# Order of the bank copies and of the late products in a hand-ordered down projection (gated linear attention layer with MLP, one Trainium2 core)

## The chip, the cores and the metric

The kernel runs on one core of a Trainium2 chip. The metric is the device time of one execution in microseconds (us); the time given for a kernel is the median of its runs. Five engines work side by side, each through its own instructions in the order in which they were queued: PE (TensorE, matrix products), DVE (VectorE) and ACT (ScalarE) for work on elements, POOL (GpSimd), and SP, which here issues the loads. They wait for one another by semaphores. PE reads its operands from SBUF, the on-chip memory of 128 partitions, and accumulates into PSUM, which has 8 banks of 128 x 512 float32.

## The reference

One layer with 256 tokens of width 2048, all in float32: RMS norm, gated linear attention, residual; RMS norm, an MLP with squared ReLU and 8192 hidden columns, residual; a last RMS norm.

```python
def _sq_relu_mlp(h, w_up, w_down):
    a = jax.nn.relu(h @ w_up)
    return (a * a) @ w_down

def reference(x, ...):
    h = x
    h = h + _gla_mixer(_rmsnorm(h, gla_norm[0]), ...)
    h = h + _sq_relu_mlp(_rmsnorm(h, mlp_norm[0]), mlp_w_up[0], mlp_w_down[0])
    return _rmsnorm(h, final_norm)
```

The change touches the product with `w_down` alone, and the final norm that follows it.

## The kernel before

**Precision.** A float32 product is made of three products of a reduced type (float32r): each operand is split into a high part, the value cast by ACT (`copy_hi`, line 110), and a low part, the rest, by DVE (`parts`, line 119): high x high, high x low, low x high. So each weight tile that comes by DMA costs ACT a cast, DVE a subtraction, and PE three times the matmuls. One matmul streams 256 columns; a load of weights goes beside the matmul before it. The split parts stand in five slots of the pool `wpool` (tags `hi` and `lo`), the raw tiles in six.

**The MLP.** The hidden columns go in 8 rounds (`ROUNDS`, m = 0 to 7) of 1024. `up` (line 679) makes the activations of a round in two passes (q = 0, 1) of 8 up steps each, into two banks that it takes from the queue `free`. An up step is one weight tile of 128 x 1024 and 24 matmuls (line 195). When a pass has ended, its `end` runs behind the first split of the next pass: `normalized` (DVE, `su`), then `forms`, which squares on ACT and writes, with DVE and ACT, up to eight stationary forms of each of the round's four pairs kp, each split into high and low part (`act`). Once in a round (`even`, step 3 of the pass q = 0) `weights` lays the two halves of an up step's weights further apart (`gap`).

`down` (line 776) adds a round's part of the second product to `h`. It goes over the output in groups g of 512 columns (`GROUPS` = 4), in an order that turns with each round, so that the last group of a round is the first of the next; consecutive passes over one group share their banks. The last round takes only groups 0 and 1 there. For each group there are four pairs kp, that is four steps, 16 in a round. A step is of one of two kinds:

- plain: one weight tile of 128 x 1024, 24 matmuls into the banks B32 and BX4, which hold the two token tiles of the group;
- by sums (`by_sums`, line 667): a 2 x 2 scheme with seven block products in place of eight, 21 matmuls. The tile's first 256 columns aren't split (so 128 x 768). Three products (9 matmuls) use the tile's own blocks. DVE makes four sums of blocks (line 821: one instruction over 512 columns, two over 256), which are split in turn, and four more products (12 matmuls) use them, into P57, P16 and BX4. P57 and P16 are banks of their own; what they hold is kept in `sums` between a group's passes, and `combine` adds it to `h` in the end.

94 steps go by sums: in the last round those with odd kp; before it all but kp = 0, and kp = 0 too where a round goes on with the group of the last one.

**Order.** The program interleaves the two generators: 18 up steps lead; then `down` yields once in each step, between its first products and those of the sums, and one up step is put in there. With 128 up steps the last ten of the 120 steps of `down` (numbers 110 to 119) have none. Each engine keeps the order that the build's scheduler gave it from the program and from `tc.issue_after`, which holds an instruction behind another: line 741 holds every copy of `copy_end` behind the last cast.

**Banks at a change of group.** Of the eight banks, four hold a group, two an up pass. In the last step of a group (`last`), ahead of its products, ACT copies `h` into two free banks for the next group's B32 and BX4 (`begin`, line 762). The old group's four banks are put into `late`. In the new group's first step by sums (kp = 1), ahead of its products, `settle` copies P16 and B32 out, into `sums` and `h`, and `begin` copies the new P16 in; behind the yield it copies P57 and BX4 out and the new P57 in. So ACT has the three copies of the first lot between the cast of that step's tile and that of the up step, and the three of the second between that and the cast of the sums. All go through line 744.

**The end.** Columns 1024 to 2047 of the last round are done behind `down`, with 8 loads of 128 x 1024 (line 911), whole token tiles as stationary operand, into five accumulators `acc`: four are begun in the last step of `down`, the fifth at kt = 1, where the last group's four banks are settled. The first two loads are used at once, the other six kept and used accumulator by accumulator. `side` and `pump` place small pieces of work (`combine`, `finish`) behind the splits.

Of the kernel before, what the change touches and what calls it, by code (L numbers as in the profile page):

```python
# [33 lines left out]
T = 256  # L34
NT = T // P
D = 2048
# [32 lines left out]
def tile_gla_mlp(ctx, tc, x, xt, cols, w_vg, w_in, w_gate, w_out, w_up, w_down, final_norm, out):  # L69
# [593 lines left out]
    def order_of(m):  # L663

        return range(GROUPS)[:: 1 if m % 2 else -1]

    def by_sums(m, g, kp):

        if m == ROUNDS - 1:
            return g < 2 and kp % 2 == 1  # L670
        return kp > 0 or m > 0 and g == order_of(m)[0]

# [58 lines left out]
    def stationary(m, kp, f):  # L731
        return [acts[m][kp // 2][:, kp % 2, i, f] for i in range(2)]
# [1 line left out]
    left, right = slice(0, T), slice(T, 2 * T)  # L734
    used, begun = set(), set()
    n_sums = [0]
    late = []

    def copy_end(to, src):

# [21 lines left out]
    def begin(k, g):  # L762
        i = free.popleft()
        bank = psum_bank(i)
        if k in (B32, BX4) or g in begun:
            copy_end(two(bank), home(k, g))
            used.add(bank.name)
        return i, bank

    def settle(n=2):  # L770

        for f in late[:n]:
            f()
        del late[:n]

    def down(passes):

        ahead = None
        for n, (m, g) in enumerate(passes):
            fresh = not n or passes[n - 1][1] != g  # L780
            if fresh:
                banks = ahead or {k: begin(k, g) for k in (B32, BX4)}
                if m == ROUNDS - 1:
                    flush()
            ends = n + 1 == len(passes) or passes[n + 1][1] != g
            for kp in range(KP):
                last = ends and kp == KP - 1
                at = lambda f: stationary(m, kp, f)

                def product(k, o, a, w, c):  # L790
# [10 lines left out]
                by_parts = by_sums(m, g, kp)  # L801
                w = parts(raw, 2 * GT, slots(), [(T * by_parts, 2 * GT)])
                if fresh and kp == 1:
                    settle()
                    banks[P16] = begin(P16, g)
                if last:
                    if n + 1 < len(passes):
                        ahead = {k: begin(k, passes[n + 1][1]) for k in (B32, BX4)}
                    else:
                        acc[0][:] = [going_on(psum_bank(free.popleft()), h[:, 0, G + lo : G + hi]) for lo, hi in cuts[0]]  # L810
                        acc[1][:] = [going_on(psum_bank(free.popleft())[:, : hi - lo], h[:, 1, G + lo : G + hi]) for lo, hi in cuts[1][:-1]]
                if by_parts:
                    block = lambda i: slice(i * T, (i + 1) * T)
# [7 lines left out]
                    add = lambda o, x, y: nc.vector.tensor_tensor(o, x, y, op=ALU.add)  # L821

                    with tc.issue_after(last_lo[0].ins):
                        add(u[:, :2], raw[:, :1].to_broadcast([P, 2, T]), raw[:, 1:3])
                        add(u[:, 2], u[:, 0], raw[:, 2])
                        last_sum[0] = add(u[:, 3], u[:, 2], raw[:, 3]).ins
                else:
                    for i in range(2):
                        for k, f in ((B32, (A11, A12)), (BX4, (A21, A22))):
                            product(k, slice(0, GT), at(f[i]), w, slice(i * GT, (i + 1) * GT))  # L830
                yield
                if fresh and kp == 1:
                    settle()
                    banks[P57] = begin(P57, g)
                if by_parts:

                    with tc.issue_after(last_lo[0].ins):
                        wu = parts(wk, G, slots())
                    product(P57, left, at(S1), wu, block(0))
                    product(P57, right, at(S3), wu, block(1))  # L840
                    product(P16, right, at(S2), wu, block(2))
                    product(BX4, right, at(A22), wu, block(3))
            if ends:

                def end(k, i, bank, g=g):
                    copy_end(home(k, g), two(bank))
                    free.append(i)

                late.extend(lambda k=k, end=end, of=banks[k]: end(k, *of) for k in range(4))
                begun.add(g)  # L850
                if m == ROUNDS - 1 or m == ROUNDS - 2 and g > 1:
                    late[-1] = lambda f=late[-1], g=g: (f(), side.extend(combine(g)))

    def combine(g):

# [9 lines left out]
            tt(1, 2, 3, ALU.subtract), tt(0, 0, 3, ALU.add), lambda: put(1),  # L865
        ]


    cuts = [HALF, [(0, 512), (512, 768), (768, 1024)]]
    acc = [[], []]  # L870
    passes = [(m, g) for m in range(ROUNDS) for g in order_of(m) if m < ROUNDS - 1 or g < 2]
    steps = up()
    for _ in range(KT + 2):
        next(steps)
    for _ in down(passes):
        next(steps, None)
# [121 lines left out]
```

## Time and profile before

| | us |
|---|---|
| median of 3 runs | 1080.33 (1080.19 to 1081.63) |
| the profiled execution | 1079.18 |
| its span, first to last instruction | 1077.1 |
| the 120 steps of `down` with the up steps among them | 432.8 to 1045.9 |
| of it the steps without an up step | from 1012.6 |
| last matmul starts | 1068.3 |
| mean granted TensorE clock | 0.998 |

Times within the execution count from the span's start. A row of a timeline gives the start, the duration, the engine, the line, the operation, what it writes and reads, how many equal instructions it stands for, and in brackets the engine's idle time before it with what ended it. Instructions of one engine overlap by their fill and drain, so the distance from start to start, and not the duration, is what one of them takes in a row of others; a matmul shows 0.28 us and the next one starts 0.113 to 0.118 us later. Ends of matmuls are modelled, and a few matmul records are missing.

### The profile page before, as it was taken

To read this page: it belongs to the slowest core of one execution; us is meant where nothing else is said; L and a number is where in the kernel's file an instruction comes from. 1 tells how busy PE (TensorE), PEld (TensorE's weight loads), DVE (VectorE), ACT (ScalarE), POOL (GpSimd) and SP (SyncE) were. 2 spreads that over 40 slices of the span, in tenths; PEclk is the share of its full clock that TensorE was granted. 3 is DMA by queue.
4 is the path that set the end of the run, shared out by engine and by line. 5 is a ranking of instruction groups with operands and counts; after the bars stand their busy time and mean duration, and the time that the engine had idled before them with its cause. 6 is when DMAs were issued, how large, how long until landed. Compare 5 with 4: busy or idle time off the path is not lost.

```text
span 1077.1 us, 22212 instructions
## 1 busy us (share of the span) xinstructions
PE 1061.8 (99%) x9148; PEld 1058.2 (98%) x9148; DVE 834.9 (78%) x1148; ACT 677.0 (63%) x917; POOL 12.8 (1%) x39
## 2 busy tenths in 40 slices
PE   9999999999999999999999999999999999999996
PEld 8999999999999999999999999999999999999986
DVE  5777645646556466898988988988989989889976
ACT  6775444545445455676686676677577667667675
POOL 0000000000000000000000000000000000000000
PEclk9999999999999999999999999999999999999999
DMA  9957765555655556556665565566566566665562
GB/s 338 321 158 214 202 193 157 154 160 176 194 183 189 181 175 193 177 179 208 218 200 196 191 217 180 195 204 209 176 197 222 183 220 195 200 198 194 172 192 107
DMA packets 94788, 210.44 MB, mean 195 GB/s; under 512 B 6704, under 2 KB 7600, under 8 KB 94560
## 3 DMA queue, kind: packets, MB, share of 16 engines
q1 hardware_dynamic: 93728, 206.99, 60.2%
q10 hardware_dynamic: 960, 2.05, 0.5%
q8 instruction: 71, 1.16, 0.4%
q14 instruction: 29, 0.24, 0.1%
HBM read 206.92 MB, written 2.10 MB: 194 GB/s over the span
## 4 chain that ended last, share of the span: by engine, by line
PE 87%; DVE 7%; issue 2%; DMA 2%; ACT 1%; SPq 0%; ACTq 0%; POOLq 0%; POOL 0%; DVEq 0%
PE acc L158 47%; PE up L195 30%; PE acc L195 6%; DVE lo L124 3%; PE aux L195 2%; DVE work L821 2%; ACT hi L114 1%; DVE lo L147 1%; DMA raw<-in_w_vg 1%; PE aux L158 1%; PE aux L564 1%; DMA zz<-in_xt 1%; PE aux L492 1%; DVE act L729 0%; DVE work L721 0%
## 5 line engine op out<-in xcount | busy, mean ns | idle before, releaser
L114 ACT CAST hi<-raw 128x1024 fp32r<-128x1024 f32 (+3 forms) x386 | 373.6, 991 | 173.8 <-PE acc L158 108.5
L158 PE MATMUL acc<-hi,act 128*128 128x256 f32 x1828 | 336.7, 278 | 4.9 <-ACT hi L114 4.8
L124 DVE TENSOR_TENSOR lo<-raw,hi 128x1024 fp32r<-128x1024 f32 (+3 forms) x226 | 246.3, 1092 | 105.7 <-ACT hi L114 105.1
L158 PEld LDWEIGHTS acc<-hi,act 128*128 128x128 f32 x1828 | 279.9, 188 | 7.1 <-ACT hi L114 7.1
L195 PE MATMUL up<-hl,hi 128*128 128x256 f32 x1024 | 280.3, 278 | 0.0
L195 PE MATMUL up<-hh,hi 128*128 128x256 f32 x1024 | 280.3, 278 | 0.0
L195 PE MATMUL up<-hh,lo 128*128 128x256 f32 x1024 | 271.4, 278 | 0.0
L147 DVE TENSOR_TENSOR lo<-raw,hi 128x1024 fp32r<-128x1024 f32 x160 | 195.0, 1220 | 61.9 <-ACT hi L114 61.2
L158 PE MATMUL acc<-lo,act 128*128 128x256 f32 x914 | 225.1, 278 | 0.0
L195 PEld LDWEIGHTS up<-hl,hi 128*128 128x128 f32 x1024 | 192.3, 188 | 0.0
L195 PEld LDWEIGHTS up<-hh,hi 128*128 128x128 f32 x1024 | 192.2, 188 | 0.0
L195 PEld LDWEIGHTS up<-hh,lo 128*128 128x128 f32 x1024 | 186.7, 188 | 0.0
L114 ACT CAST hi<-work 128x1024 fp32r<-128x1024 f32 x94 | 99.5, 1058 | 107.7 <-DVE work L821 95.6
L158 PEld LDWEIGHTS acc<-lo,act 128*128 128x128 f32 x914 | 162.8, 188 | 0.2 <-DVE lo L124 0.2
L124 DVE TENSOR_TENSOR lo<-work,hi 128x1024 fp32r<-128x1024 f32 x94 | 114.8, 1221 | 24.8 <-ACT hi L114 23.4
L158 PE MATMUL acc<-hi,xA 128*128 128x256 f32 (+1 forms) x736 | 104.9, 279 | 0.7 <-ACT hi L114 0.7
L158 PEld LDWEIGHTS acc<-hi,xA 128*128 128x128 f32 x736 | 93.7, 188 | 1.4 <-ACT hi L114 1.4
L821 DVE TENSOR_TENSOR work<-work,raw 128x256 f32<-128x256 f32 x188 | 79.5, 423 | 4.5
L821 DVE TENSOR_TENSOR work<-raw 128x512 f32<-128x512 f32 x94 | 64.3, 684 | 0.0
L158 PE MATMUL acc<-lo,xA 128*128 128x256 f32 (+1 forms) x368 | 58.5, 278 | 0.1
L744 ACT COPY sums<-acc 128x512 f32<-128x512 f32 x46 | 27.3, 594 | 47.6 <-PE acc L158 47.6
L158 PEld LDWEIGHTS acc<-lo,xA 128*128 128x128 f32 x368 | 49.6, 188 | 0.3 <-DVE lo L124 0.3
(154 smaller groups left out, 1125.7 us busy)
## 6 DMA issues: line engine op xcount, KB each, us to landing
raw<-in_w_up SPq DMA_DIRECT2D x128, 512.0 KB, 4.6
raw<-in_w_down SPq DMA_DIRECT2D x128, 512.0 KB, 3.9
raw<-in_w_in SPq DMA_DIRECT2D x80, 512.0 KB, 3.7
raw<-in_w_out SPq DMA_DIRECT2D x32, 512.0 KB, 3.6
raw<-in_w_vg SPq DMA_DIRECT2D x14, 520.0 KB, 8.5
h<-in_x SPq DMA_DIRECT2D x4, 512.0 KB, 8.8
zz<-in_xt SPq DMA_DIRECT2D x3, 384.0 KB, 8.5
fb<-in_final_norm ACTq DMA_DIRECT2D x1, 1024.0 KB, 5.5
```

Of the source, the lines that this page charges most:

```text
L114: last_hi[0] = nc.scalar.copy(to, raw)
L124: last_lo[0] = nc.vector.tensor_tensor(lo[:, s], raw[:, s], hi[:, s].bitcast(F32), op=ALU.subtract)
L147: last_lo[0] = nc.vector.tensor_tensor(to[1], dst, to[0].bitcast(F32), op=ALU.subtract)
L158: nc.tensor.matmul(o[:, m], x, w[:, m], start=first and c == 0, stop=last, skip_group_check=True)
L195: nc.tensor.matmul(o, u[:, i, s], m, start=kt == 0 and n == 0 and j % 2 == 0, stop=kt == KT - 1 and n == 2, skip_group_check=True,)
L492: nc.tensor.matmul(o, kab[:, k[0], c0 + c, k[1] : k[1] + P], q(qt[:, c0 + c]), start=c == 0, stop=c == 1)
L564: nc.tensor.transpose(b[:, o + t * P : o + (t + 1) * P], src[:, t, kt * P : (kt + 1) * P], ident)
L744: last_end[0] = nc.scalar.copy(to, src).ins
L821: add = lambda o, x, y: nc.vector.tensor_tensor(o, x, y, op=ALU.add)
```

## The change

`by_sums` names other steps. In the last round (0, 0), (0, 2) and (1, 2), as pairs of g and kp, go by sums in place of four; in the round before it the last group's kp = 3 no longer does. `LEAD` and `UPS` count the up steps. The two lists `cuts` and `acc` move up, and `last_banks` begins a token tile's accumulators.

The part of a step behind the yield is a function now, `of_sums`. Where an up step stood in the yield, it runs at once, as before. Where none does, it is kept in `pending`, and runs in the next step behind that step's first products, ahead of its yield.

The copies at a change of group stand elsewhere. `late` is a dictionary by bank. `first` is the new group's first step by sums. Behind the yield of the step before it, P16 is copied out and the new P16 in; behind the yield of the step itself, P57 likewise; behind its sums' products, B32 and BX4 are copied out. The copies in for the next group's B32 and BX4 go from ahead of the last step's products to behind its yield. Since a copy is held behind the last cast, a copy behind the yield stands on ACT behind the cast of the up step's tile.

At the end two accumulators are begun in the last step of `down`, two at the first load, the fifth at the second; the last group's banks are copied out one by one at the second to fifth load.

```diff
     def by_sums(m, g, kp):
         if m == ROUNDS - 1:
-            return g < 2 and kp % 2 == 1
+            return (g, kp) in ((0, 0), (0, 2), (1, 2))
+        if m == ROUNDS - 2 and g == order_of(m)[-1]:
+            return kp in (1, 2)
         return kp > 0 or m > 0 and g == order_of(m)[0]
+
+    LEAD = KT + 2
+    UPS = ROUNDS * MR // GT * KT // 2
...
-    late = []
+    late = {}
...
-    def settle(n=2):
-        for f in late[:n]:
-            f()
-        del late[:n]
+    def last_banks(t, cs=slice(0, 2)):
+        for lo, hi in cuts[t][cs]:
+            acc[t].append(going_on(psum_bank(free.popleft())[:, : hi - lo], h[:, t, G + lo : G + hi]))
+
+    def settle(*ks):
+        for k in ks:
+            late.pop(k, lambda: None)()
...
+            first = min(kp for kp in range(KP) if by_sums(m, g, kp)) if fresh else None
             for kp in range(KP):
...
-                if fresh and kp == 1:
-                    settle()
-                    banks[P16] = begin(P16, g)
-                if last:
-                    if n + 1 < len(passes):
-                        ahead = {k: begin(k, passes[n + 1][1]) for k in (B32, BX4)}
-                    else:
-                        acc[0][:] = [going_on(psum_bank(free.popleft()), h[:, 0, G + lo : G + hi]) for lo, hi in cuts[0]]
-                        acc[1][:] = [going_on(psum_bank(free.popleft())[:, : hi - lo], h[:, 1, G + lo : G + hi]) for lo, hi in cuts[1][:-1]]
...
+                if pending:
+                    pending()
+                    pending = None
                 yield
-                if fresh and kp == 1:
-                    settle()
-                    banks[P57] = begin(P57, g)
-                if by_parts:
+                def of_sums(wk=wk if by_parts else None, product=product, at=at):
                     with tc.issue_after(last_lo[0].ins):
                         wu = parts(wk, G, slots())
                     product(P57, left, at(S1), wu, block(0))
                     product(P57, right, at(S3), wu, block(1))
                     product(P16, right, at(S2), wu, block(2))
                     product(BX4, right, at(A22), wu, block(3))
+                if fresh and kp == first - 1:
+                    settle(P16)
+                    banks[P16] = begin(P16, g)
+                if fresh and kp == first:
+                    settle(P57)
+                    banks[P57] = begin(P57, g)
+                if last:
+                    if n + 1 < len(passes):
+                        ahead = {k: begin(k, passes[n + 1][1]) for k in (B32, BX4)}
+                    else:
+                        last_banks(0)
+                if by_parts:
+                    if units + LEAD < UPS:
+                        of_sums()
+                    else:
+                        pending = of_sums
+                units += 1
+                if fresh and kp == first:
+                    settle(B32, BX4)
...
     for kt in range(KL):
...
+        if kt == 0:
+            last_banks(1)
+        elif kt == 1:
+            settle(P16)
+        elif kt <= KL - LAST + 2:
+            settle((P57, B32, BX4)[kt - 2])
+            if not late:
+                side.extend([lambda t=t: finish(t, 512, 512) for t in range(NT)])
...
             if kt == 1:
-                settle()
-                acc[1].append(going_on(psum_bank(free.popleft())[:, :T], h[:, 1, D - T :]))
-                settle()
-                side.extend([lambda t=t: finish(t, 512, 512) for t in range(NT)])
+                last_banks(1, slice(2, 3))
                 for k, v in enumerate((first, w)):
                     last_step(k, v, 1, 2)
```

In the built programs ACT's order at the change of group of step 29 (s: a step's tile by sums, p: a plain one, U: an up step's, W: the sums', by number of the step) is:

```
before: p28 U46 s29 | out P16, out B32, in P16 | U47 | out P57, out BX4, in P57 | W29 s30 U48 W30
after:  p28 U46 | out P16, in P16 | s29 U47 | out P57, in P57 | W29 | out B32, out BX4 | s30 U48 W30
```

DVE's order there is the same in both. PE's order in the last steps, with the number of matmuls:

```
before: s109x9 U127x24 W109x12 s110x9 W110x3 s111 W110x9 s111x8 W111x3 p112x2 W111x9 p112x2 s113 p112x20 s113x8 W113x3 ...
after:  s109x9 U127x4 W109x3 U127x20 W109x9 s110x2 p111x2 s110x7 p111x22 W110x3 s112 W110x9 s112 p113x2 s112x7 p113x22 W112x3 ...
```

The program before has 9114 matmuls and transposes, the one after 9120; both have 184 copies of this kind.

More of the change, by code (lines that the diff above doesn't have):

```diff
@@ L768, in begin @@
         return i, bank
-    def settle(n=2):
-        for f in late[:n]:
-            f()
-        del late[:n]
+    cuts = [HALF, [(0, 512), (512, 768), (768, 1024)]]
+    acc = [[], []]
+    def last_banks(t, cs=slice(0, 2)):
[4 more added lines that the diff above has]
+            late.pop(k, lambda: None)()
     def down(passes):
-        ahead = None
+        ahead = pending = None
+        units = 0
         for n, (m, g) in enumerate(passes):
@@ L785, in down, with product @@
             ends = n + 1 == len(passes) or passes[n + 1][1] != g
+            first = min(kp for kp in range(KP) if by_sums(m, g, kp)) if fresh else None
             for kp in range(KP):
                 last = ends and kp == KP - 1
[L788 to L790 removed]
+                by_parts = by_sums(m, g, kp)
+                def product(k, o, a, w, c, banks=banks, last=last):
                     bank = banks[k][1]
@@ L847, in end @@
                     free.append(i)
-                late.extend(lambda k=k, end=end, of=banks[k]: end(k, *of) for k in range(4))
+                late.update({k: lambda k=k, end=end, of=banks[k]: end(k, *of) for k in range(4)})
                 begun.add(g)
                 if m == ROUNDS - 1 or m == ROUNDS - 2 and g > 1:
-                    late[-1] = lambda f=late[-1], g=g: (f(), side.extend(combine(g)))
+                    late[BX4] = lambda f=late[BX4], g=g: (f(), side.extend(combine(g)))
     def combine(g):
@@ L866, in combine @@
         ]
-    cuts = [HALF, [(0, 512), (512, 768), (768, 1024)]]
-    acc = [[], []]
     passes = [(m, g) for m in range(ROUNDS) for g in order_of(m) if m < ROUNDS - 1 or g < 2]
     steps = up()
-    for _ in range(KT + 2):
+    for _ in range(LEAD):
         next(steps)
```

4 lines of the change are left out of this document (2 added, 2 removed).

## The prediction

> **What bounds the kernel now.** I read the page first, then the busy time of PE over stretches of the down projection, then the timelines of ACT, DVE and PE around one change of group and around the last ten steps.
>
> ```profile
> span 1077.1 us, 22212 instructions
> PE 1061.8 (99%) x9148; PEld 1058.2 (98%) x9148; DVE 834.9 (78%) x1148; ACT 677.0 (63%) x917; POOL 12.8 (1%) x39
> ```
>
> PE is the bound: of 1077.1 us it is idle for 15. That leaves two things to win or lose: its waits, and the pace of a matmul. The second shows when the matmuls of a stretch are counted (columns: stretch, its length, PE busy and number of matmuls, granted clock, DMA share, GB/s):
>
> ```profile
> 442.00:599.60 157.60, 157.60 (x1392) 1.00 0.61 200
> 611.00:778.80 167.80, 167.80 (x1425) 1.00 0.62 199
> 779.80:854.70 74.90, 74.90 (x663) 1.00 0.62 199
> 863.00:938.10 75.10, 74.94 (x661) 1.00 0.62 201
> 949.50:1011.00 61.50, 61.50 (x523) 1.00 0.62 206
> 1011.10:1045.90 34.80, 30.35 (x237) 1.00 0.48 152
> 1045.90:1068.50 22.60, 22.60 (x193) 1.00 0.30 105
> ```
>
> The same 256-column matmul comes every 157.6/1392 = 113.2 ns in the first row and every 167.8/1425 = 117.75 ns in the second, 4.0% slower, both at a granted clock of 1.00. The third and fourth rows are fast again (113.0 and 113.6), the fifth is slow (117.6). I call this the fast and the slow pace. In the sixth row, where the up steps are over, 237 matmuls at 117.75 ns would take 27.9 us of 34.8: 6.9 us are waits. The seventh has none.
>
> I number the steps of `down` by u (16 a round, the last ten are 110 to 119); p28 is a plain step's weights, s29 a step by sums', W29 its sums' part (the products P57, P16 and BX4 behind the yield), U47 up step 47. I matched the trace to these by each engine's program order. Step 29 is the first by sums of a new group. What ACT and DVE do there:
>
> ```profile
> 574.32 1.78 ACT L114 CAST hi<-raw 128x1024 fp32r<-128x1024 f32 x2
> 578.17 0.59 ACT L744 COPY sums<-acc 128x512 f32<-128x512 f32 x1 [2.08 <-PE acc L158]
> 578.66 0.59 ACT L744 COPY h<-acc 128x512 f32<-128x512 f32 x1
> 579.13 0.61 ACT L744 COPY acc<-sums 128x512 f32<-128x512 f32 x1
> 579.65 1.06 ACT L114 CAST hi<-raw 128x1024 fp32r<-128x1024 f32 x1
> ...
> 582.08 1.08 ACT L114 CAST hi<-work 128x1024 fp32r<-128x1024 f32 x1
> ```
>
> ```profile
> 575.78 1.22 DVE L147 TENSOR_TENSOR lo<-raw,hi 128x1024 fp32r<-128x1024 f32 x1
> 576.92 0.95 DVE L124 TENSOR_TENSOR lo<-raw,hi 128x768 fp32r<-128x768 f32 x1
> 577.79 0.68 DVE L821 TENSOR_TENSOR work<-raw 128x512 f32<-128x512 f32 x1
> 578.51 0.89 DVE L821 TENSOR_TENSOR work<-work,raw 128x256 f32<-128x256 f32 x2
> 580.75 1.23 DVE L147 TENSOR_TENSOR lo<-raw,hi 128x1024 fp32r<-128x1024 f32 x1 [1.35 <-ACT hi L114]
> 583.19 1.23 DVE L124 TENSOR_TENSOR lo<-work,hi 128x1024 fp32r<-128x1024 f32 x1 [1.21 <-ACT hi L114]
> 584.33 0.95 DVE L124 TENSOR_TENSOR lo<-raw,hi 128x768 fp32r<-128x768 f32 x1
> 587.85 1.28 DVE L708 SCALAR_TENSOR_TENSOR su<-up,work 128x512 f32<-128x512 f32 x2
> ```
>
> ```profile
> 583.20:610.80 27.60, 27.36 (x40) 1.00 0.53 173
> ```
>
> ACT casts U46 and s29 at 574.3 and 575.3 (the first row's two), then stands 2.08 us at the copy of P16's bank into `sums`, until PE has ended W27's product in that bank. Three copies go by, U47's high part, three more copies, W29's high part, s30's. DVE idles for 1.35 and 1.21 us meanwhile. The last row is DVE's own busy time over the next 27.6 us: 27.36, that is 99%. From step 30 to 34, five steps by sums with the end of an up pass among them, DVE never catches up; what it is late at 584.33 it is late at 610.8. There PE meets it:
>
> ```profile
> 609.74 1.05 ACT L114 CAST hi<-work 128x1024 fp32r<-128x1024 f32 x1 [2.91 <-DVE work L821]
> 610.84 0.39 PE L158 MATMUL acc<-hi,act 128*128 128x256 f32 x1 [0.16 <-ACT hi L114]
> 567.60 1.05 ACT L114 CAST hi<-work 128x1024 fp32r<-128x1024 f32 x1 [2.15 <-DVE work L821]
> 569.02 0.50 PE L158 MATMUL acc<-hi,act 128*128 128x256 f32 x3
> 695.14 1.06 ACT L114 CAST hi<-work 128x1024 fp32r<-128x1024 f32 x1 [2.90 <-DVE work L821]
> 696.73 0.40 PE L158 MATMUL acc<-hi,act 128*128 128x256 f32 x2
> 525.64 1.05 ACT L114 CAST hi<-work 128x1024 fp32r<-128x1024 f32 x1 [2.89 <-DVE work L821]
> 527.43 0.62 PE L158 MATMUL acc<-hi,act 128*128 128x256 f32 x4
> ```
>
> W34's high part is ready at 610.79, and PE's matmul starts at 610.84; the one before it started at 610.41, so 0.44 less a step of 0.113: 0.32 us are lost. The next pair is W26, with 0.37 us to spare at the fast pace (ready 568.65, used 569.02); the third is W50, 0.64 to spare at the slow pace (ready 696.20, used by the second of the row's two, 696.84); the last is W18, 0.85 to spare at the fast pace (ready 526.69, used by the second of the four, 527.54). After 610.84 PE runs slow until 778.8 (rows of the first table). Step 98 has the same wait, and behind it stands the slow stretch from 949.5. A wait so tends to leave PE at the slow pace; the step whose weights lie apart (`gap`, once a round) tends to end it, as ahead of 779.8. At step 82, within the fast row of 863 to 938.1 (its idle 0.16 is this wait), it did not.
>
> **The change, part by part.** *Which steps go by sums.* 92 steps instead of 94, each 21 matmuls against 24: 6 more matmuls, at 117.75 ns +0.7 us. DVE loses two sums with their low parts, 1.61 and 1.14 us each by the rows above; both lie in the last ten steps and are in the tail's sum.
>
> *Copies at a change of group.* Their number stays. By the new program order ACT goes: U46, copy out of P16, copy in of P16, s29, U47, copy out and in of P57, W29, copies out of B32 and BX4, s30. Behind the copy that waits for PE now stands s29, which had been done three us ahead. Worked forward with the rows' start-to-start times (a copy 0.48 to 0.52, a 768-column cast 0.73, a 1024-column one 0.95): the copies at 578.17 and 578.66, s29 from 579.18 to 580.0, U47 at 579.9, two copies to 581.9. DVE, idle since 577.0, starts s29's low part at 580.05 instead of 576.92, its sums end 2.5 us later, 582.5 (0.87 and the two rows' 1.61); U47's low part takes it to 583.7. ACT casts W29 from 582.55 to 583.6, two copies take it to 584.5, s30 ends at 585.35. DVE starts s30 at 585.4 against 584.33: **1.05 us later**. PE has other work until 583.2 and waits for nothing here; it waits five steps on. At the middle change of a round (step 25, with forms in between) the same walk gives 0.75. At step 13, where nothing is copied in, it gives 1.5: the copy out at 494.91 as now, then s13, U31, a copy, W13, two copies and s14, whose low part starts at 501.55 in place of the second row's time:
>
> ```profile
> 494.91 0.59 ACT L744 COPY sums<-acc 128x512 f32<-128x512 f32 x1 [2.86 <-PE acc L158]
> 500.03 0.95 DVE L124 TENSOR_TENSOR lo<-raw,hi 128x768 fp32r<-128x768 f32 x1
> ```
>
> So at the fast pace a round gets these waits: at W26 0.75 - 0.37 = 0.4; at the last change 0.32 + 1.05 = 1.4; 1.8 together. At the slow pace W26's counterpart comes out about even, since PE takes 4% longer from the copy to that use, and W50's 0.64 turns into a wait of 0.4. Rounds 1 to 6 have it; the first meets it at W18, at 527.5 us, where 1.5 late meets 0.85 to spare.
>
> From there I take PE to go slow for good, but for some 3 us a round behind the widely laid step. Newly slow are then 599.6 - 527.5 = 72.1, 74.9 and 75.1 us, less 18: 204 us x 4.0% = **+8.2**. The waits themselves are six of 0.4 in place of three of 0.35: **+1.4**. Bounds: no rate change and no wait, 0; or 1.8 us in each of six rounds with no rate won or lost, +10.8.
>
> The cover of the other moved copies: those in of B32 and BX4 go behind the up step's high part in the step where the group ends; DVE has the sums before them to do (1.61 us), which hides both copies. Without it, they would cost 1.0 a group. The last round's forms that grow from 896 to 1024 columns add 0.15 twice, in the slow stretch.
>
> *The last ten steps.* Products of a sum follow the next step's 24 plain matmuls. Now the rows of this place:
>
> ```profile
> PE acc L158 <- ACT hi L114: 4.4, 8, 1.7
> 1018.25 0.62 PE L158 MATMUL acc<-hi,act 128*128 128x256 f32 x3 [1.73 <-ACT hi L114]
> 1010.65 0.69 DVE L708 SCALAR_TENSOR_TENSOR su<-up,work 128x512 f32<-128x512 f32 x1 [0.43 <-PE up L195]
> 1016.98 1.07 DVE L721 TENSOR_TENSOR work<-work 128x256 f32<-128x256 f32 x3
> 1015.59 0.68 DVE L729 TENSOR_TENSOR act<-work,act 128x512 fp32r<-128x512 f32 x1
> 1021.98 1.22 DVE L729 TENSOR_TENSOR act<-work,act 128x1024 fp32r<-128x1024 f32 x1
> ```
>
> PE waits for the high part of sums eight times, 1.73 us the longest; with the pipe's refill and smaller ones that is the 6.9 us above. In the new order DVE sets the end. From `su` at 1011.0 (three of W109's matmuls now stand inside U127: 0.35 later): `su` 0.6, p111 1.14, `su` 0.6, the rest of 110's sums 0.8 and the forms' differences 0.8, 1014.9; the cast of W110 and its low part, 1016.8; s112 0.87, a sum 0.6, p113 1.14, the forms' 1.14, two sums 0.9, 1021.5; the second forms' cast and low part, 1022.5; W112 behind its cast, 1024.0; s114 0.87, a sum 0.6, p115 1.14, sums 0.9, 1027.5; W114's cast 1.05 and low part 1.14, 1029.8. PE without a wait starts s110 at 1012.57 and wants that low part 123 matmuls later, 1027.1. So 2.7 us of waits stay, at W112 and W114. Behind it the plain steps 116 and 117 (48 matmuls, 5.65 us) cover the last sum. The tail gains 6.9 - 2.7 - 0.7 = **3.5**; bounds 6.2 (no wait left) and 2.
>
> The final copies out, now spread over five loads, stand behind casts which PE uses 5 us later; the seventh row (193 matmuls, no wait) is their cover. Without it they'd cost their four copies, 2 us.
>
> *Sum.* The profiled execution took 1079.2 (span 1077.1 and 2.1 around it), 1.15 below the median of the three runs, 1080.33: I leave this as noise. 1079.2 + 8.2 + 1.4 - 3.5 = **1085.3**.
>
> The Trainium skill (TensorE: Matmul & The Clock Gate, Back-to-back issue gap) gives a warm matmul one spacing, N/2.4 + 2.5 ns, an estimate of 109.2 at 256 columns. The trace disagrees: 113.2 and 117.75 at one granted clock. By that rule a wait would cost itself alone, and the term of 8.2 would fall away; this is the second rival.
>
> **The rivals.** *Faster: the late casts find room.* It is decided at W34 and its like: if s30's low part comes less than 0.4 us later than now, no new wait arises and the pace stays as it is. For it: two of DVE's idle pieces were ACT's six copies, of which only four now stand ahead of W29. Against: the copy that waits for PE stands ahead of s29 in the queue. Main part 0, tail -3.5 to -6.2: 1073 to 1075.7.
>
> *The pace doesn't follow the waits.* For it: the wait of step 82, behind which PE stayed fast. The stretches keep their pace of now and the waits come on top: rounds 1, 2, 5 and 6 mostly fast with 1.8 less today's 0.35 in three of them, two slow ones with 0.4: 7.2 - 1.05 + 0.8 = +7; 1079.2 + 7 - 3.5 = 1082.7. If every restart fell into the fast pace instead, the slow rows ahead of the tail, 229 us x 4%, would give 9 back, and all six rounds would pay 1.8: 1079.2 - 9 + 10.8 - 1.05 - 3.5 = 1076.5.
>
> *The late products don't do what they say.* If DVE is 2.5 us later still at 1014.9, as it would be with 110's sums queued behind the forms, the waits of the tail come back: gain 1, and with the first case's main part 1087.8.
>
> **How the numbers follow.** The forecast has 0.48, the faster case 0.25, the pace that doesn't follow 0.17, the tail without gain 0.10. A measurement of this kernel tells 0.2%, 2.2 us, from no change: below 1078.2 faster, above 1082.5 slower. Slower: 0.43 of the first, 0.08 of the pace's case and 0.09 of the last, 0.60; faster: the faster case and 0.03 of the pace's, 0.28; the rest, 0.12, the same. The range for 8 in 10 goes from inside the faster case, 1074, to above the tail without gain, 1089; the forecast's own is 1082.5 to 1088.
>
> **What would show it.** Right: at each first step by sums of a group ACT idles some 3 us ahead of that step's cast and DVE starts the next step's low part about 1 us later against PE; PE waits at W18 and then takes 117.8 ns a matmul up to 599; in the last ten steps waits of some 2.7 us, at W112 and W114. Wrong: 113.2 ns in the stretches that have it now, or PE's waits for ACT in rounds 1 to 6 not above today's three.

## The result, and the profile after

The changed kernel takes 1090.20 us (1090.10 to 1090.94, 4 runs) against 1080.26 (1079.37 to 1081.63, 4 runs): ratio 1.0092, 95% interval 1.0075 to 1.011, slower by 0.9%. The forecast of 1085.3 had the sign and the place, but half the size, and the time lies 1.2 above the range.

The first lines of the page after:

```profile
span 1088.1 us, 22191 instructions
PE 1074.5 (99%) x9154; PEld 1069.0 (98%) x9154; DVE 830.7 (76%) x1140; ACT 678.0 (62%) x915; POOL 12.8 (1%) x39
```

DVE has 4 us less to do than before, ACT 1 us more and PE six matmuls more; but the span is 11.0 us longer. The busy time of PE by stretches says where (columns as before: stretch, its length, PE busy and its matmuls, weight loads, DVE, ACT, POOL, granted clock, DMA share, GB/s; a window also counts the two or three matmuls that its edges cut, so a short one reads up to 1% low):

```profile
442.00:485.50 43.50, 43.50 (x387) 43.50 (x386) 35.88 (x50) 28.88 (x38) 0.00 (x0) 1.00 0.59 190
487.00:523.00 36.00, 36.00 (x308) 36.00 (x307) 32.46 (x47) 22.97 (x29) 0.00 (x0) 1.00 0.61 201
...
660.50:684.50 24.00, 24.00 (x214) 24.00 (x213) 20.23 (x29) 15.53 (x21) 0.00 (x0) 1.00 0.64 212
703.50:778.00 74.50, 74.50 (x633) 74.29 (x632) 64.09 (x88) 51.94 (x69) 0.00 (x0) 1.00 0.61 197
...
432.60:1026.92 594.32, 591.83 (x5019) 588.00 (x5017) 522.97 (x713) 405.29 (x523) 0.00 (x0) 1.00 0.60 194
1026.92:1079.90 52.98, 51.21 (x422) 49.85 (x420) 42.51 (x63) 36.05 (x59) 0.55 (x1) 1.00 0.42 147
```

Before:

```profile
432.75:1012.57 579.82, 579.35 (x5018) 578.76 (x5017) 523.10 (x715) 402.43 (x523) 0.00 (x0) 1.00 0.61 198
1012.57:1068.90 56.33, 51.55 (x416) 49.47 (x414) 46.57 (x68) 37.84 (x62) 0.55 (x1) 1.00 0.42 139
```

From the first matmul of `down` to that of step 110 (below: the main part) the same matmuls take 594.3 us in place of 579.8. The first two stretches show the pace turning from 112.4 ns a matmul (43.5/387) to 116.9 at 486; most of what follows is slow (74.5/633 = 117.7), some of it fast again (24/214 = 112.1).

I split the main part by the distances from one matmul's start to the next in the trace: what a distance over 135 ns has above 118 ns is a wait; the rest belongs to the fast pace (113.33 ns) or to the slow one (117.78) by the median of its neighbours. The tail runs from the first matmul of step 110 to the start of the last one.

| | before | after | difference | forecast |
|---|---|---|---|---|
| waits in the main part | 1.4 | 7.7 | +6.3 | +1.4 |
| time at the slow pace | 258.6 | 470.9 | | |
| time at the fast pace | 318.6 | 110.4 | 208.2 x 3.93% = +8.2 | +8.2 |
| tail | 55.7 | 52.4 | -3.3 | -3.5 |

The three differences, and 0.15 less ahead of `down`, are the 11 us of the spans. The profile's own view of PE's waits counts only part of them (wait, total us, times, longest); the main part and the tail of the kernel after:

```profile
PE acc L158 <- ACT hi L114: 1.9, 8, 0.4
...
PE acc L158 <- ACT hi L114: 0.9, 1, 0.9
PE acc L158 <- DVE lo L124: 0.4, 2, 0.2
```

Nearly all of these waits are for the split of sums. ACT's timeline at step 29, the place that the prediction walked through:

```profile
581.95 0.59 ACT L750 COPY sums<-acc 128x512 f32<-128x512 f32 x1 [2.95 <-PE acc L158]
582.57 0.59 ACT L750 COPY acc<-sums 128x512 f32<-128x512 f32 x1
583.09 1.78 ACT L114 CAST hi<-raw 128x768 fp32r<-128x768 f32 x2
584.78 0.58 ACT L750 COPY sums<-acc 128x512 f32<-128x512 f32 x1
585.38 0.59 ACT L750 COPY acc<-sums 128x512 f32<-128x512 f32 x1
586.80 1.05 ACT L114 CAST hi<-work 128x1024 fp32r<-128x1024 f32 x1 [0.83 <-DVE work L830]
587.76 1.06 ACT L750 COPY h<-acc 128x512 f32<-128x512 f32 x2
588.71 1.79 ACT L114 CAST hi<-raw 128x768 fp32r<-128x768 f32 x2
```

and DVE's:

```profile
583.95 0.96 DVE L124 TENSOR_TENSOR lo<-raw,hi 128x768 fp32r<-128x768 f32 x1 [3.32 <-ACT hi L114]
...
587.88 1.23 DVE L124 TENSOR_TENSOR lo<-work,hi 128x1024 fp32r<-128x1024 f32 x1 [0.31 <-ACT hi L114]
589.59 0.96 DVE L124 TENSOR_TENSOR lo<-raw,hi 128x768 fp32r<-128x768 f32 x1 [0.48 <-ACT hi L114]
```

The cast of s29 now stands behind the copy that waits 2.95 us for PE, and DVE idles 3.32 us for it. I measure lateness from that copy, since PE sets its start: step 30's low part starts 7.64 us behind it (589.59 - 581.95), before 6.16 (584.33 - 578.17). So DVE is 1.48 us later than before at step 29, and 1.21 at the same change of the later rounds (7.36 against 6.15).

### The profile page after: what moved, and what is told of

It is laid out like the page before. It is cut to its first block, busy times and chain, and to the rows that moved or that the text cites. A ratio compares the mean times of both kernels' runs of the same rounds, so it can differ in the third digit from the quotient of the medians.

```text
span 1088.1 us, 22191 instructions
## 1 busy us (share of the span) xinstructions
PE 1074.5 (99%) x9154; PEld 1069.0 (98%) x9154; DVE 830.7 (76%) x1140; ACT 678.0 (62%) x915; POOL 12.8 (1%) x39
## 3 DMA queue, kind: packets, MB, share of 16 engines
q1 hardware_dynamic: 93728, 206.99, 59.4%
## 4 chain that ended last, share of the span: by engine, by line
PE 80%; DVE 12%; issue 3%; ACT 3%; DMA 2%; SPq 0%; ACTq 0%; POOLq 0%; POOL 0%; DVEq 0%
PE acc L158 44%; PE up L195 25%; PE acc L195 6%; DVE lo L124 5%; DVE work L830 3%; PE aux L195 2%; DVE lo L147 2%; ACT hi L114 2%; DMA raw<-in_w_vg 1%; PE aux L158 1%; PE aux L564 1%; DVE act L735 1%; DMA zz<-in_xt 1%; PE aux L492 1%; DVE work L727 1%
## 5 line engine op out<-in xcount | busy, mean ns | idle before, releaser
L158 PE MATMUL acc<-hi,act 128*128 128x256 f32 x1832 | 341.5, 281 | 3.5 <-ACT hi L114 2.8
L114 ACT CAST hi<-work 128x1024 fp32r<-128x1024 f32 x92 | 96.8, 1053 | 116.2 <-DVE work L830 111.1
L124 DVE TENSOR_TENSOR lo<-work,hi 128x1024 fp32r<-128x1024 f32 x92 | 112.4, 1222 | 4.8 <-ACT hi L114 2.8
```

What stands on the lines that cost most here:

```text
L114: last_hi[0] = nc.scalar.copy(to, raw)
L124: last_lo[0] = nc.vector.tensor_tensor(lo[:, s], raw[:, s], hi[:, s].bitcast(F32), op=ALU.subtract)
L158: nc.tensor.matmul(o[:, m], x, w[:, m], start=first and c == 0, stop=last, skip_group_check=True)
```

## The experiments

None of the kernels below leaves out any of the reference's work; e8, e11 and e12 do one cast twice. "Late" is the start of the second by-sums step's low part behind P16's copy out, at step 29 (at step 61 in brackets). The before of a run is that of the same chip.

| run | us | before | ratio (95%) | late | main part | waits in it | slow pace in it | tail |
|---|---|---|---|---|---|---|---|---|
| before | 1080.33 | | 1 | 6.16 (6.15) | 579.8 | 1.4 | 259 | 55.7 |
| after | 1090.20 | 1080.26 | 1.0075 to 1.011 | 7.64 (7.36) | 594.3 | 7.7 | 471 | 52.4 |
| e1 copies as before | 1074.64 | 1079.67 | 0.9932 to 0.9961 | 6.15 (6.15) | 581.2 | 0.9 | 309 | 50.0 |
| e2 copies alone | 1096.39 | 1079.67 | 1.0129 to 1.0163 | | 595.2 | 9.9 | 436 | 59.4 |
| e3 B32, BX4 later | 1082.11 | 1079.67 | 1.0014 to 1.0037 | 7.08 (6.81) | 587.4 | 2.3 | 436 | 52.4 |
| e7 P16 back | 1074.03 | 1078.23 | 0.9942 to 0.9972 | 6.02 (6.02) | 580.2 | 1.0 | 278 | 50.8 |
| e6 both | 1061.55 | 1078.23 | 0.983 to 0.986 | 5.46 (5.46) | 569.0 | 0.0 | 10 | 49.6 |
| e9 e6, products as before | 1066.08 | 1080.33 | 0.9853 to 0.9882 | | 569.0 | 0.0 | 10 | 54.8 |
| e10 e6 without `gap` | 1061.61 | 1080.33 | 0.9812 to 0.9841 | | 568.5 | 0.0 | 0 | 49.6 |
| e11 e10 and one cast | 1080.28 | 1080.33 | 0.9987 to 1.0006 | | 586.6 | 2.9 | 403 | 50.8 |
| e12 e6 and one cast | 1068.83 | 1080.33 | 0.9874 to 0.9903 | | 574.8 | 2.8 | 88 | 50.8 |
| e5 before without `gap` | 1083.89 | 1078.23 | 1.0035 to 1.0065 | | 584.6 | 0.4 | 417 | 55.7 |
| e8 before and one cast | 1084.19 | 1078.23 | 1.003 to 1.0065 | | 584.7 | 3.5 | 330 | 56.0 |
| e4 before, two `gap` steps | 1078.34 | 1079.67 | 0.9968 to 0.9992 | | 579.6 | 1.3 | 250 | 55.2 |

### Which part of the change costs

**e1, the copies as before.** The edit of the changed kernel:

```diff
+                if fresh and kp == first:
+                    settle(P16, B32)
+                    banks[P16] = begin(P16, g)
...
-                if fresh and kp == first - 1:
-                    settle(P16)
-                    banks[P16] = begin(P16, g)
                 if fresh and kp == first:
-                    settle(P57)
+                    settle(P57, BX4)
                     banks[P57] = begin(P57, g)
...
-                if fresh and kp == first:
-                    settle(B32, BX4)
```

The first three lines stand behind the cast of the step's tile; the begin of the next group's banks goes back ahead of the last step's products.

> The changed kernel with the copies at a change of group put back where they stood before (P16, B32 and BX4's ahead of the first by-sums step's first product or behind the yield, as before); the late products and the end of the changed kernel stay. Theory (the copies' place makes the waits and the slow pace of the down projection, the late products win the tail): from the first matmul of the down projection to s110 579.7 us as before (changed kernel 594.2), waits of 1.4 us in it, some 319 us of it at 113 ns a matmul; the tail 52.2 as after; the time 1080.3 - 3.5 = 1076.8. Rival (the slow stretches come from something else in the change, the copies only stand beside it): main part stays near 594, the time 1088 to 1091.

```profile
433.02:1014.24 581.22, 581.02 (x5018) 580.62 (x5017) 523.90 (x716) 402.96 (x523) 0.00 (x0) 1.00 0.62 198
1014.24:1064.90 50.66, 50.20 (x422) 49.61 (x420) 41.26 (x60) 36.21 (x59) 0.55 (x1) 1.00 0.44 154
```

The main part is back at 581.2, so the copies' place makes 13.1 of the 14.5 us that it lost. The other 1.4 are 50 us more at the slow pace than before's 259 (1.9), less 0.5 of waits. The tail is shorter than expected: 50.0 where I had 52.2. The late products alone win 5.7 us, and the moved copies take 2.4 of that back.

**e2, the copies alone** (the sums' products right behind their step, `by_sums` as before):

```diff
-                    if units + LEAD < UPS:
-                        of_sums()
-                    else:
-                        pending = of_sums
+                    of_sums()
```

> The change without its late products: the sums' products stand right behind their step again, which steps go by sums is as before; the copies and the end stand as in the changed kernel. Theory: main part 594 us and its waits 7.7 as after; the tail 55.7 as before with its waits of 7; the time 1090.2 + 3.5 = 1093.7. Rival (the late products cost it, the copies nothing): 1080 to 1082.

```profile
433.19:1028.39 595.20, 590.69 (x5019) 586.87 (x5017) 522.93 (x714) 404.76 (x523) 0.00 (x0) 1.00 0.60 193
1028.39:1088.40 60.01, 54.39 (x416) 52.33 (x414) 47.72 (x73) 39.52 (x65) 0.55 (x1) 0.94 0.40 130
```

The main part is within 0.9 us of the changed kernel's. The time came out 2.7 above the forecast: the tail is 3.7 longer than before's. Most of that isn't the copies'. The tail's row has a granted clock of 0.94: from 1036.8 to 1040.0 us and from 1057.9 to 1060.5 the trace gives a clock of 0.50, and the matmuls there start 213 ns apart in place of 118. These 30 matmuls cost some 2.8 of the 3.7 us.

**e3, B32 and BX4 later, and e7, P16 back.** Each moves one pair of copies in the changed kernel. e3 puts the copies out of B32 and BX4 behind the next step's cast:

```diff
+                if fresh and kp == first + 1:
+                    settle(B32, BX4)
...
-                if fresh and kp == first:
-                    settle(B32, BX4)
```

> The changed kernel with the copies out of B32 and BX4 one step later, behind the cast of the next step's tile, which then doesn't wait for them. Theory (ACT's work ahead of that cast makes DVE late): the cast comes about 0.5 to 1.0 us earlier, the waits of the main part fall from 7.7 us to 2.5 to 5; the pace stays slow, since small waits stay; the time 1083 to 1088. Rival (DVE is late by the wait for PE alone, at the copy ahead of s29's cast): waits 7.7 and 1090 as after. Second rival (the pace is lost in proportion to the waits): with waits near 3, half of the 208 us come back, 1081.

e7 puts P16's pair behind the cast of the first step by sums:

```diff
+                if fresh and kp == first:
+                    settle(P16)
+                    banks[P16] = begin(P16, g)
...
-                if fresh and kp == first - 1:
-                    settle(P16)
-                    banks[P16] = begin(P16, g)
```

> The changed kernel with only P16's two copies put back behind the cast of the first by-sums step's tile; those of B32 and BX4 stay ahead of the next step's cast. Theory (the wait for PE ahead of s29's cast is most of the lateness): waits of the main part fall from 7.7 us to 2 or less, time 1077 to 1082. Rival (B32 and BX4 make most of it, as the run with these later suggests with 5.4 us of waits won): waits stay above 3 us and the time above 1083.

e3 makes DVE 0.56 us earlier and takes 5.4 us of the 7.7 of waits away, but the slow pace stays (436 us), and the time is 1082.1, one below its range. That time lies near the 1081 of the second rival, but the way there doesn't: 35 us come back to the fast pace, not half of the 208. So the pace isn't lost in proportion to the waits. e7 makes DVE 1.62 us earlier (1.34 at step 61), leaves 1.0 us of waits, and lands at 1074.0, below its range: the tail's 50.8 shows that most of the copies' loss there goes too. Either edit alone removes most of the waits, so their 7.7 us can't be shared out between the two pairs: each wait is lateness above a use's spare time, and both pairs feed the same lateness.

**e6, both edits.**

> The changed kernel with P16's copies behind the cast of the first by-sums step's tile, as before, and the copies out of B32 and BX4 behind the cast of the step after it; late products and end as in the changed kernel. Theory (what ACT does ahead of these two casts sets DVE's lateness five steps on): DVE about 0.7 us earlier than before, no wait at W34, W66, W98, perhaps none at W32 either; main part without waits (1.4 us less than before), more of it at the fast pace than before's 319 us: between 319 and 577, 0 to 10 us less; tail 50 as in the run with the copies as before: 1079.7 - 1.4 - 5.7 = 1072.6 at most, 1063 at best. Rival (the pace is what it is without waits too): 1073 to 1075.

ACT at step 29, and DVE's next low part:

```profile
577.05 0.59 ACT L750 COPY sums<-acc 128x512 f32<-128x512 f32 x1 [2.75 <-PE acc L158]
...
580.28 1.05 ACT L114 CAST hi<-work 128x1024 fp32r<-128x1024 f32 x1
581.23 0.83 ACT L114 CAST hi<-raw 128x768 fp32r<-128x768 f32 x1
581.96 1.06 ACT L750 COPY h<-acc 128x512 f32<-128x512 f32 x2
```

```profile
582.50 0.95 DVE L124 TENSOR_TENSOR lo<-raw,hi 128x768 fp32r<-128x768 f32 x1
```

The cast of step 30 (581.23) stands ahead of the two copies now; 582.50 - 577.05 = 5.45, that is 0.7 earlier than before (6.16), as expected. What this does to PE:

```profile
524.00:605.00 81.00, 81.00 (x717) 81.00 (x716) 73.47 (x101) 59.94 (x77) 0.00 (x0) 1.00 0.63 201
606.00:770.00 164.00, 164.00 (x1448) 164.00 (x1447) 151.00 (x208) 119.10 (x154) 0.00 (x0) 1.00 0.63 203
...
432.07:1001.11 569.04, 569.04 (x5018) 569.04 (x5017) 523.65 (x716) 407.54 (x523) 0.00 (x0) 1.00 0.64 202
1001.11:1051.20 50.09, 49.23 (x422) 48.16 (x420) 40.99 (x60) 35.93 (x58) 0.55 (x1) 1.00 0.45 153
```

In the main part there is not one wait, and the fast pace holds from end to end (164/1448 = 113.3 ns); the 10 us that the table counts as slow are the widely laid steps' own matmuls, some ten a round at 120 ns. The tail still has waits. The time is 1061.55 us, 1.5% less than the kernel before (ratio 0.9845, 95% interval 0.983 to 0.986) and 2.4% less than the changed one (1061.55/1078.23 over 1090.20/1080.26). The 0.7 us at each change of group bring 10.8 us in the main part. Of them 1.4 are waits; the rest is pace. With e10 below it is the best version found.

**e9, e6 with the products of before** (the edit of e2 on e6).

> The run with the best copies (1061.55 us), its sums' products standing right behind their step again and the same steps by sums as before: the copies alone, in the good place. Theory (copies and late products are worth their own terms): main part 569 us without a wait, at the fast pace; tail as before with its 7 us of waits, 55.7 or, at the fast pace, 54: 1061.6 + 4.5 to 6 = 1066 to 1068. Rival (the late products are what keeps the main part free of waits): waits in the main part again and 1075 or more.

The main part is the same 569.0, the tail 54.8. So the parts of the change hold apart: well placed copies 10.8 us, late products 5.2.

### What sets the pace

**e4, a second `gap` step a round, and e5, none,** in the kernel before:

```diff
-                even = (6,) if m == q == 0 else (0,) if m == 0 else (3,) if q == 0 else ()
+                even = (6,) if m == q == 0 else (0,) if m == 0 else (3, 5) if q == 0 else ()
```

> The kernel before with one edit: a second up step a round (s % 16 == 5) in the first pass has its weights laid apart, as that of s % 16 == 3 has, so that it stands two steps later. Theory (the widely laid step returns PE to the fast pace, a wait tends to leave it slow, and where the first one fails a second one may succeed): the slow stretches from 611 to 778 and from 949 to 1011 get shorter, 0 to 9 us less, 1071 to 1080 and none longer. Rival (the pace follows neither the waits nor this step): the stretches stay where they are or move at random, 1080. Second rival (a widely laid step costs DVE and ACT time): new waits behind it, 1081 to 1083.

```diff
-                even = (6,) if m == q == 0 else (0,) if m == 0 else (3,) if q == 0 else ()
+                even = (6,) if m == q == 0 else (0,) if m == 0 else ()
```

> The kernel before with no up step laid apart after the first round. Theory (once a wait has left PE at the slow pace, only a widely laid step can bring it back): fast until the first wait at the end of the second up pass (about 600 us), then 117.8 ns a matmul to the end; fast time in the main part 318.6 us down to about 167, 152 us x 4% = 6: 1079.7 + 6 = 1086. Rival (the pace comes back by itself or follows something else, as the groups or the DMA): fast stretches stay, 1080.

e4 gives little: of eight widely laid steps that PE reached slow, three left it fast (606, 617, 776, 786 and 946 didn't; before: four of five). The time is 0.2% less, and in the profiled execution 250 us are slow in place of 259. The slow stretches moved rather than shrank: PE is slow from 769 to 863 us, where before it was fast from 780 on. So e4 speaks for its first rival (the stretches move, 1080) as much as for the theory. e5 came as forecast, 5.7 us more:

```profile
450.00:599.00 149.00, 149.00 (x1317) 149.00 (x1316) 134.12 (x184) 103.12 (x134) 0.00 (x0) 1.00 0.63 199
612.00:1017.00 405.00, 405.00 (x3441) 405.00 (x3440) 361.37 (x496) 279.27 (x367) 0.00 (x0) 1.00 0.62 198
```

Fast (113.1) up to the first wait at 600, slow (117.7) for all the 405 us behind it, though it has only 0.4 us of waits.

**e10, e6 without `gap`.**

> The run with the best copies, and no up step laid apart after the first round. Theory (the widely laid step only brings PE back to the fast pace after a wait; without a wait nothing needs it): fast throughout, 1061 to 1062. Rival (the fast pace needs that step once a round): slow from about 600, 20 us more.

```profile
617.00:1000.00 383.00, 383.00 (x3382) 383.00 (x3381) 354.45 (x488) 277.33 (x360) 0.00 (x0) 1.00 0.63 205
```

383/3382 = 113.2: where nothing waits, the fast pace needs no help.

**e11, e12 and e8, one cast more.** The high part of one step's sums is cast twice, in e10, e6 and the kernel before (there at step 18):

```diff
-                        wu = parts(wk, G, slots())
+                        wu = slots()
+                        if n * KP + kp == 34:
+                            copy_hi(wu[0][:, :G], wk)
+                        wu = parts(wk, G, wu)
```

> The run with the best copies and no step laid apart, and the high part of the sums of step 34 cast twice: one ACT copy of 0.95 us more, against 0.59 us to spare, so that PE waits once, about 0.4 us, at 609.6 us. Theory (one wait leaves PE at the slow pace, and nothing brings it back): 117.8 ns a matmul from 609.6 to the end, some 3800 matmuls x 4.4 ns = 17: 1061.6 + 0.4 + 17 = 1079. Rival (a wait costs itself): 1062.

> The same late cast at step 34 in the run with the best copies, whose widely laid step stands once a round. Theory: slow from 609.6 to the first widely laid step that brings the fast pace back, at 688, 771 or 853: 3.1, 6.4 or 9.7 us and 0.4 for the wait: 1065 to 1072, most likely 1065. Rival (a wait costs itself): 1062.

> The kernel before with one edit: the high part of the sums of step 18 is cast twice, one ACT copy of 0.95 us in the whole program more, so that PE waits once, some 0.1 to 0.3 us, at 527.5 in a fast stretch. Theory (a wait of any length leaves PE at the slow pace till the next widely laid step): 117.8 ns a matmul from 527.5 to 600, +2.8 us and the wait: 1079.7 + 3.0 = 1082.7, and the stretches behind 606 may fall otherwise (up to 3 us each way). Rival (the wait costs itself alone): 113.3 ns stays, 1079.9.

PE's timeline of e11 at the place, and its stretches:

```profile
612.98 0.62 PE L158 MATMUL acc<-hi,act 128*128 128x256 f32 x3 [0.21 <-ACT hi L114]
614.24 0.39 PE L158 MATMUL acc<-lo,act 128*128 128x256 f32 x1 [0.64 <-DVE lo L124]
...
617.77 0.62 PE L158 MATMUL acc<-hi,act 128*128 128x256 f32 x3 [1.25 <-ACT hi L114]
```

```profile
525.00:612.00 87.00, 87.00 (x770) 87.00 (x769) 76.72 (x105) 63.15 (x83) 0.00 (x0) 1.00 0.63 203
617.00:1019.00 402.00, 401.23 (x3406) 401.24 (x3407) 360.24 (x492) 283.57 (x365) 0.00 (x0) 1.00 0.61 198
```

The one cast makes three waits, not the one that I expected: the high part, the low part behind it, and the next sums. Together 2.9 us. But the kernel takes 1080.3 in place of 1061.6: from 613 on each matmul takes 117.8 ns, to the end. Some 17 of the 19 us are the pace (403 us slow in the main part, and 41 more than e10 in the tail, x 3.8%); the waits make 2.5 (2.9 here, 0.4 less than e10's in the tail). e12, with a widely laid step at 695, pays this for 83 us only and gets the fast pace back there:

```profile
620.00:694.00 74.00, 74.00 (x631) 74.00 (x630) 66.48 (x93) 53.52 (x69) 0.00 (x0) 1.00 0.62 201
696.00:1000.00 304.00, 304.00 (x2683) 304.00 (x2682) 281.19 (x386) 220.70 (x286) 0.00 (x0) 1.00 0.64 204
```

e8 came out 6.0 above its before where I had 3.0: again three waits, not one of 0.2, so 2.2 us more of waits than before has, and 71 us more at the slow pace, 2.8. The theory of the pace holds in all three; the number of waits was underestimated each time.

## Why the prediction was wrong

**The waits at changes of group, +1.4, is the term that failed; they took 6.3.** The prediction walked one change through and asked which use would wait. Four things in it were off:

- The lateness. "1.05 us later" was 1.48 at step 29 and 1.21 further on; at the middle change of a round the 0.75 was 0.93 (7.66 against 6.73). Two steps of the walk were too short. The copy into P16's bank starts 0.62 us behind the copy out of it (582.57 - 581.95), where the walk took 0.48 to 0.52, the distance of copies in different banks; s29's low part so starts 2.00 us behind the copy out, where the walk had 1.88. And the cast of W29 waits until DVE's sums have ended: it starts 2.85 us behind that low part (586.80 - 583.95), where the walk added DVE's start-to-start times to 2.5. P57's copies, 0.60 apart, don't count: ACT stands idle for these sums behind them (0.83).
- The uses. It held the lateness against W18, W26, W34 and W50 only. W31 and W32, between them, had 0.75 and 0.13 us to spare before, and the 0.13 were none in effect: W32's second matmul came 30 ns late already then, at 600.1 us, just behind the first table's fast row. After the change W31, W32 and W34 all wait, as W47, W48 and W50 do a round on: 19 uses of sums' high parts in the main part, where "six of 0.4" were forecast. Over these 19, what their distance from the matmul ahead has above 118 ns adds up to 5.5 us. Of these, W34 and its like (W50, W66, W82, W98), which the prediction had in view, make 1.5, and W18 adds 0.1: less than its 2.4. The rest is of uses that it didn't look at or took to come out even.
- The slow pace. "At the slow pace W26's counterpart comes out about even" missed that a wait can also leave PE fast: behind the waits at W42 (659.5 us) and W74 (832.9) PE was fast for 26 us each, and the uses then came earlier than the walk at the slow pace had them. W47 and W79 waited 0.5 us, the longest of their rounds.
- The restart. At each of the 19 the second matmul starts 0.22 us behind the first, not 0.118; 19 times 0.106 make 2.0 of the other 2.2 us of the 7.7. The prediction counted such a refill in the tail, and not here.

**The pace, +8.2, came out as forecast, partly by luck.** PE turned slow at 486 us, 41 earlier than "at 527.5": W10, of a change that the prediction hadn't walked, waited some 30 ns, and that was enough (three matmuls start to end in 0.54 us, where the fast pace gives 0.50; behind them the steps are 0.12):

```profile
486.06 0.28 PE L195 MATMUL up<-hl,hi 128*128 128x256 f32 x1
486.17 0.54 PE L158 MATMUL acc<-hi,act 128*128 128x256 f32 x3
486.55 0.28 PE L195 MATMUL up<-hh,lo 128*128 128x256 f32 x1
486.67 0.28 PE L195 MATMUL up<-hh,hi 128*128 128x256 f32 x1
```

Against it stand the two stretches of 26 us at the fast pace. The mechanism is shown: e11 and e12 make waits and get the slow pace to the end or to the next widely laid step; e6 and e10 have none in the main part and run fast there.

**The tail, -3.5, was right in its sum (-3.3) and wrong in its shares.** The prediction left 2.7 us of waits at W112 and W114 to DVE's own work; by the split above the changed kernel has 3.2 in the tail. e1, with the same products and the copies of before, has 0.7 left, so DVE nearly keeps up, and 2.5 of the 3.2 are due to the copies' place. Part of that is the last change's lateness: the changed kernel's DVE starts s110's low part 3.15 us ahead of PE's step 110, e1's 4.36. It is not all: e7, whose DVE is as early as before at the changes, keeps 1.4. What makes these wasn't tried. So the near sum was partly luck.

**The rivals.** "The late casts find room" fell: it asked for less than 0.4 us of lateness, and there were 1.2 to 1.5 at W34's change. But room there is: e6 finds it. "The pace doesn't follow the waits" fell with e5, e10 and e11; with it fell a single warm spacing, by which e11's cast would have cost its waits of 2.9 us and not 19. The Trainium skill (TensorE: Matmul & The Clock Gate, Back-to-back issue gap) gives the formula that the prediction took from it for isolated matmuls; for streams of loads and matmuls it has figures at 128 and 512 columns alone. So "the trace disagrees" went too far: 113.33 and 117.78 ns are spacings of a stream. "The late products don't do what they say" fell with e1 (5.7 us won) and e9 (5.2).

The change so consists of a good part, the late products, and a misplaced one. Taking six copies two by two was not the fault; standing ahead of the casts of s29 and s30 was.

## What to carry to other kernels

Where PE has two paces, a wait's price is not its length: look, behind each wait, at the distance from matmul to matmul up to the next event that resets it, and value a change by whether any wait is left. When an engine is made late, hold the lateness against every later use and its spare time, not against the tightest one of before. A copy that waits for PE, or that nobody needs soon, goes behind the casts that feed the next engine.

## What the runs showed of the hardware

PE runs the same stream of loads and 256-column matmuls at either of two steady spacings, 113.33 or 117.78 ns, at one granted clock of 1.00. A wait of 30 ns is enough to go from the lower to the higher one. In the main parts of all 14 traces the pace turns slow at a wait (a distance over 135 ns) and nowhere else: of 49 waits that PE met fast, 44 left it slow and five fast. It turns fast again at a widely laid step (30 of the 47 met slow) or, four times, at a wait. Without a wait the lower held for 568 us (e10), and the higher one held for the 405 us of e5's second row. A step whose weights lie further apart left the fast pace fast each time (e6) and turned the slow one fast in four cases of five (before) or three of eight (e4); what decides it is open, as is why a few waits leave PE fast and what the two spacings are inside PE. Stretches that fall one way in one execution and the other in the next may be why runs of the kernel before spread over 1076.5 to 1081.9 on one chip; that was not tried.
